# A hybrid gMLP/SSD layer on one core: rounded A parts kept in HBM, y's transposes and stores placed later, and the last three steps of the output projection run tile by tile

## The chip, the core and the metric

One core of a Trainium2 chip runs one launch of the kernel. The metric is the device time of an execution in microseconds (us); less is better. The engines are called as in the profile: PE (TensorE: matrix products and transposes), DVE (VectorE), ACT (ScalarE), POOL (GpSimd) and SP (SyncE, which issues every transfer of this kernel).

## What is computed

`x` is 2048 tokens by 1024 features, float32. The reference, cut to what matters here:

```python
h = rms_norm(x, pre_w)
proj = einsum('bld,dc->blc', h, w_in)            # 1024 -> 6160 columns
u, v, zg, z, xbc, dt_raw = split(proj)
# group A, 8 heads of 128: spatial gating in chunks of 128 tokens
s   = einsum('hts,bcshd->bcthd', tril(ws), layer_norm(v)) + bs
y_a = grouped_rms_norm(u * s * silu(zg), gmlp_norm_w, 128)
# group B, 16 heads of 64: causal conv, SiLU, Mamba-2 scan in chunks of 128
y   = y_diag + y_off + xs * d_skip
y_b = grouped_rms_norm(y * silu(z), ssd_norm_w, 256)
mixed = einsum('blc,cd->bld', concat([y_a, y_b]), w_out)   # 2048 -> 1024
out = x + rms_norm(mixed, post_w)
```

## The kernel before, in words

**Products.** The input projection is done as six units of 1024 columns (u = 0 to 5 in `UNITS`: xbc, z, xbc, v, u/zg, u/zg), the output projection as unit 6. Tokens are cut into four blocks of T = 512, handled as two pairs (`PAIRS`, p = 0 and 1); a block and half of the contraction is a quarter of a 2x2 block product, and each pair is done with seven products instead of eight (Winograd's form of Strassen's scheme): `PRODS` P1 to P7. The left operand A of a product is either a plain quarter of the activations (P1, P2, P4: `PLAIN_A`) or a sum or difference of quarters (P6, P7, P5, P3); the right operand B comes in the same way from the weights.

**Steps and tiles.** A step is one product on one slice j of the contraction: 28 steps in each of units 0 to 5, 56 in unit 6, 224 in all. A step runs over four tiles c of 128 rows; a tile is two calls of `mm3`, that is six products of 128x128 by 128x512. `mm3` gives fp32 accuracy from rounded parts: each operand is split into a part rounded to fp32r ("hi") and the rest ("lo"), and hi·hi, hi·lo and lo·hi are added. `split` (lines 157 to 162) makes the two parts of a 128x1024 piece: one ACT copy (line 160) and one DVE subtraction (line 161).

**Where A comes from.** `make_a` (line 720) makes the A of a step. In unit 0 it loads and combines pieces, splits them, and for the combined products stores both parts (1 MB) in HBM, in `a_d` (line 776). Units 1 to 5 use the same activations: for the combined products they load both parts from `a_d` with one 1 MB transfer into a buffer of `apool` (line 732); for the plain products they load the 0.5 MB piece into a buffer of `rpool` and split it once more (lines 724 to 728). Unit 6 works on y and splits everything. `look_ahead` (line 829) makes the A of step i+2 and the B of step i+3 while step i runs. `apool` has 3 buffers, `bpool` 5, `rpool` 7.

**Beside the products.** `run_tasks` advances generators between the tiles; `now` counts 1.36 per tile (`RUN`), and a generator says with `yield n` how much later it is due. The longest one is `ssd_stream` (line 474): 16 rounds, one for each block and head group, of which one has the transposes of x, B and C into a PSUM bank (`tok_x`, `tok_b`), the decays and exponentials on ACT, four chunks (`chunk`: products, state, y), and a norm. The normalised y of a round is turned by `y_tiles` (line 546): two times four PE transposes into one of the three banks of pool `ps`, an ACT copy out of it (line 554), and a store. In the kernel before these two parts of the round before are run at lines 504 and 512, between `tok_x(1)`, `tok_b` and the next decays. For group A `gate_out` (line 621) normalises with ACT, waits 8, and runs `y_tiles`.

**Accumulators.** Pool `pj` has five PSUM banks; `after` (line 864) empties or copies an accumulator when a product's last slice is done (line 872 is ACT's copy of P1 in mid-accumulation, lines 876 to 901 are DVE's, line 614 is ACT's SiLU).

**Stores.** `store` puts a store in a list and `flush` issues it on SP once `now` has moved on by `BEHIND` = 2.7, that is two tiles.

**Order.** The kernel is built with a scheduler that orders each engine's instructions by a simulated time line, with the program's order as priority: PE's tiles of a step may be taken in mixed order when one part of an operand is late, and SP's transfers can move. On the chip each engine then works through its own list in that order.

**The end.** The last product of unit 6 is P3 of pair 1, four steps (j = 0 to 3). `use_o` (line 672) takes each finished tile: sum of squares on ACT, times the weight on DVE, then (second half of a row) reciprocal root of the mean on POOL (line 173), two DVE operations on the two halves (line 689), and two stores. `bring` (line 695) loads what these need, tile by tile in the step before the last one (line 932).

Of the kernel before, what the change touches and what calls it, by code (L numbers as in the profile page):

```python
# [8 lines left out]
F32 = mybir.dt.float32  # L9
# [6 lines left out]
P = 128  # L16
# [11 lines left out]
EPS = 1e-6  # L28
RUN = 1.36
SPACE = 2.5  # L30
BEHIND = 2.7
LOOK_A = 2
LOOK_B = 3

# [17 lines left out]
def hybrid_kernel(ctx: ExitStack, tc: tile.TileContext, x, x_t, pre_w, w_u, w_o, w_dt,  # L52
# [27 lines left out]
    def rt(name):  # L80
# [2 lines left out]

    hd = [[dram.tile([P, 2, T], F32, name=f"hd{b}_{j}") for j in range(4)] for b in range(NB)]
    a_d = [{(m, j): dram.tile([P, 2, 2, T], F32, name=f"as{p}{m}{j}") for m in PRODS for j in range(2)
            if m not in PLAIN_A} for p in range(2)]
    s_d = {(p, m, j): dram.tile([P, 2, T], F32, name=f"s{p}{m}{j}") for p in range(2) for m in ("S2", "S3")
           for j in range(4)}
    t3_d = [dram.tile([P, 2, T], F32, name=f"t3{j}") for j in range(4)]
# [67 lines left out]
    def split(pool, name, t):  # L157

        w = pool.tile([P, 2, 2, T], F32R, name=name)
        nc.scalar.activation(w[:, :, 0, :], t, AF.Copy)  # L160
        nc.vector.tensor_tensor(w[:, :, 1, :], t, w[:, :, 0, :], ALU.subtract)  # L161
        return w
# [39 lines left out]
    def spawn(gen, delay=0):  # L202
        task = [now[0] + delay, gen]
        tasks.append(task)
        if delay == 0:
            advance(task)
        return task
# [19 lines left out]
    def flush(until):  # L227
        while stores and stores[0][0] <= until:
            _, dst, src, then = stores.pop(0)
            nc.sync.dma_start(out=dst, in_=src)  # L230
            if then:
                then()
# [241 lines left out]
    def ssd_stream():  # L474
        order = [(b, 2 * u + n) for u in range(2) for n in range(2) for b in range(NB)]

        def ready(b, g):
            return all((bb, g) in raw_in for bb in range(b + 1))

        cur, prev = Ssd(*order[0]), None  # L480
        for i in range(4):
            cur.load_raw(i)
            if i % 2:
                yield 5
                cur.conv(i - 1)
                yield 0
                cur.conv(i)
                yield 0
        cur.silus()
        for n in range(len(order) + 1):  # L490
            nxt = Ssd(*order[n + 1]) if n + 1 < len(order) else None
            if nxt:
                while not ready(nxt.b, nxt.g):
                    yield 5
            if cur:
                while (cur.b, cur.g // 2) not in zs_in:
                    yield 5
                for c in range(NT):
                    cur.load_e(c)
                cur.tok_x(0)  # L500
                yield 0
                cur.tok_x(1)
            if prev:
                next(prev.out, None)
            yield 0
            if cur:
                cur.tok_b()
                cur.decay(0)
                cur.decay(1)
                yield 0  # L510
            if prev:
                next(prev.out, None)
            if not cur:
                return
            if nxt:
                nxt.load_raw(0)
            cur.load_z(0)
            cur.decay(2)
            cur.decay(3)
            yield 0  # L520
            cur.exps()
            cur.load_z(1)
            yield 0
            cur.operands(0)
            yield 0
            for c in range(NT):
                if nxt:
                    nxt.conv(c)
                    if c + 1 < NT:
                        nxt.load_raw(c + 1)  # L530
                yield 0
                if c + 1 < NT:
                    cur.operands(c + 1)
                cur.chunk(c)
                if c + 2 < NT:
                    cur.load_z(c + 2)
                yield 0
            if nxt:
                nxt.silus()
            cur.norm()  # L540
            yield 0
            prev, cur = cur, nxt
# [78 lines left out]
    def gate_out(b, hp):  # L621
        yg, ss = gate[b, hp], g_ss[b, hp]
        r = rsqrt_mean(ss[:, :, :].rearrange("p c i -> p (c i)"), NT * 2, 1.0 / P, "g")
        for c in range(NT):
            for i in range(2):
                nc.scalar.activation(yg[c][:, i * P:(i + 1) * P], yg[c][:, i * P:(i + 1) * P], AF.Copy,  # L626
                                     scale=r[:, 2 * c + i:2 * c + i + 1])
        yield 8
        yield from y_tiles(b, yg, hp)


# [88 lines left out]
    def make_a(u, p, name, j):  # L720

        piece = lambda m, k: a_piece(u, p, m, k, j)
        tt = nc.vector.tensor_tensor
        if name in PLAIN_A:
            t, = load([piece(*PLAIN_A[name])])
            yield
            yield split(apool, "a", t)
            return
        if 0 < u < 6:
            yield  # L730
            w = apool.tile([P, 2, 2, T], F32R, name="a")
            nc.sync.dma_start(out=w[:, :, :, :].bitcast(F32), in_=a_d[p][name, j][:, :, :, :])
            yield w
            return
        if u == 0:
            yield
        if name == "P6":
            if u == 0:
                t, q, r = load([piece(0, 0), piece(1, 0), piece(1, 1)])
                tt(t, t, q, ALU.subtract)  # L740
                s3_in[p, j] = t
                tt(r, r, t, ALU.subtract)
                s2 = s2_in[p, j] = [gt("s2") for _ in range(2)]
                for kk in range(2):
                    nc.gpsimd.tensor_copy(s2[kk], r[:, kk, :])
                t = r
            else:
                q, t = load([piece(1, 1), s_d[p, "S3", j]])
                yield
                tt(t, q, t, ALU.subtract)  # L750
                store(s_d[p, "S2", j], t)
        elif name == "P7":
            if u == 0:
                t = s3_in.pop((p, j))
            else:
                t, q = load([piece(0, 0), piece(1, 0)])
                yield
                tt(t, t, q, ALU.subtract)  # L758
                store(s_d[p, "S3", j], t)
        elif name == "P5":  # L760
            t, q = load([piece(1, 0), piece(1, 1)])
            if u:
                yield
            tt(t, t, q, ALU.add)  # L764
        elif u == 0:
            t, = load([piece(0, 1)])
            s2 = s2_in.pop((p, j))
            for kk in range(2):
                tt(t[:, kk, :], t[:, kk, :], s2[kk], ALU.subtract)
        else:  # L770
            t, q = load([piece(0, 1), s_d[p, "S2", j]])
            yield
            tt(t, t, q, ALU.subtract)
        w = split(apool, "a", t)
        if u == 0:
            store(a_d[p][name, j], w[:, :, :, :].bitcast(F32))
        yield w
# [133 lines left out]
    spawn(prep(1), 1)  # L911
    spawn(prep(2), 16)
    spawn(prep(3), 30)
    accs = {}
    for i, (u, p, name, j, first, fin) in enumerate(steps):
        _, channels, _, nj = UNITS[u]
        at = i - 28 * u
        if at == 0:
            if u == 1:
                spawn(ssd_stream(), 4)  # L920
            if u == 3:
                row_w["v"] = row_weights(v_w)
            if u == 6:
                row_w["post"] = row_weights(post_w)
        for uu in (4, 5):
            for b, n, w in WANTED:
                if i == uu * 28 + w - 5:
                    spatial_task[b, 2 * (uu - 4) + n] = spawn(spatial(b, 2 * (uu - 4) + n), 1)
        look_ahead(i)
        A, B = made_a.pop(i), made_b[u, name, j]  # L930
        for c in range(NT):
            if u == 6 and name in ("P3", "P5") and j == nj - 2:
                bring(PAIRS[p][name == "P5"], c)
            if first:
                accs[c] = pj.tile([P, T], F32, name="acc", tag="pj")
            cs = slice(c * P, (c + 1) * P)
            for kk in range(2):
                a, b_ = A[:, kk], B[:, kk]
                st, en = first and kk == 0, fin and kk == 1
                if channels:  # L940
                    m = mm3(accs[c], b_[:, 0, cs], b_[:, 1, cs], a[:, 0, :], a[:, 1, :], st, en)
                else:
                    m = mm3(accs[c], a[:, 0, cs], a[:, 1, cs], b_[:, 0, :], b_[:, 1, :], st, en)
            step_end[:] = [m.ins]
            now[0] += RUN
            if j == nj - 1:
                after(u, p, name, c, accs[c])
            with tc.issue_after(step_end[0]):
                flush(now[0])
            run_tasks()  # L950
    assert not tasks
    flush(now[0] + 99)

# [41 lines left out]
```

## Time and profile before

| | |
|---|---|
| median of 3 runs | 1606.11 us (1606.04 to 1612.49) |
| profiled execution | 1609.79 us, of which 1608.0 us from first to last instruction (span) |
| PE busy | 1515.3 us, 94% of the span |
| DVE, ACT, POOL busy | 70%, 54%, 25% |
| transfers | 456.88 MB, mean 284 GB/s |

The units of the product loop begin at about 37, 248, 441, 642, 854, 1072 and 1279 us. The profile lists busy time by engine, a granted TensorE clock (1.00 is 2.4 GHz, 0.50 is 1.2 GHz), the waits of each engine with what released them, and the chain that ended last. A wait costs time only where it holds the engine that bounds the kernel, or something that engine will need.

### The profile page before, as it was taken

Reading aid. Unit: us, or ns where it says so; the run is one execution under the profiler, and the core shown is the slowest. Engines: PE = TensorE matmul, PEld = TensorE weight load, DVE = VectorE, ACT = ScalarE, POOL = GpSimd, SP = SyncE. Lnnn points to the kernel's source line nnn. Section 1 sums busy time; section 2 is a strip of 40 time slices with the busy share of each in tenths; the row PEclk is TensorE's granted clock in tenths of the full one; section 3 lists DMA queues with packets and bytes.
Section 4 is the critical chain, followed back from the end, with each engine's and each line's share of the span. In section 5 each row is a group of like instructions: output and inputs, shape, how many; then the busy total and the mean of one; then the engine's idle time right before and its main releaser. Section 6 shows DMA issues by size and latency. Waiting matters only on the chain. (4 is left out here: it accounts for less than half of the span.)

```text
span 1608.0 us, 21653 instructions
## 1 busy us (share of the span) xinstructions
PE 1515.3 (94%) x7268; PEld 1259.7 (78%) x7268; DVE 1129.0 (70%) x1756; ACT 870.8 (54%) x1823; POOL 408.7 (25%) x449
## 2 busy tenths in 40 slices
PE   4979999999989999999899899998999999999996
PEld 4768888778778888778778788787888887888875
DVE  4466876677676687677778669696676645687698
ACT  4431325666576654665466765879647743333332
POOL 1000000323332333342224434364624300000022
PEclk9987999999999999999999999999999999999998
DMA  8699999968788697786787776757866689797998
GB/s 334 251 365 348 334 416 337 343 224 285 273 274 291 222 328 273 255 300 238 259 285 233 251 268 217 260 175 250 293 222 233 216 278 331 259 380 247 336 357 327
DMA packets 159119, 456.88 MB, mean 284 GB/s; under 512 B 18848, under 2 KB 35616, under 8 KB 146720
## 3 DMA queue, kind: packets, MB, share of 16 engines
q1 hardware_dynamic: 159008, 455.51, 80.2%
q8 instruction: 57, 0.93, 0.2%
q14 instruction: 54, 0.44, 0.1%
HBM read 348.35 MB, written 107.09 MB: 283 GB/s over the span
## 5 line engine op out<-in xcount | busy, mean ns | idle before, releaser
L165 PE MATMUL acc<-b,a 128*128 128x512 f32 x1344 | 543.4, 405 | 19.7 <-ACT sg L614 4.9
L167 PE MATMUL acc<-b,a 128*128 128x512 f32 x1344 | 526.4, 396 | 4.6 <-DVE a L161 4.2
L166 PE MATMUL acc<-b,a 128*128 128x512 f32 x1344 | 528.7, 393 | 0.0
L165 PEld LDWEIGHTS acc<-b,a 128*128 128x128 f32 x1344 | 254.4, 189 | 75.0 <-ACT sg L614 5.5
L167 PEld LDWEIGHTS acc<-b,a 128*128 128x128 f32 x1344 | 254.1, 189 | 60.1 <-DVE a L161 5.9
L166 PEld LDWEIGHTS acc<-b,a 128*128 128x128 f32 x1344 | 254.9, 190 | 49.7
L160 ACT ACTIVATE a<-r 128x1024 fp32r<-128x1024 f32 x144 | 151.8, 1056 | 242.1 <-PE acc L167 115.6
L161 DVE TENSOR_TENSOR a<-r,a 128x1024 fp32r<-128x1024 f32 x144 | 179.0, 1244 | 70.1 <-ACT a L160 69.7
L165 PE MATMUL acc<-a,b 128*128 128x512 f32 x448 | 182.5, 415 | 16.6 <-ACT b L160 5.8
L372 DVE SCALAR_TENSOR_TENSOR cv_out<-cv_raw,cw,cv_out 128x512 f32<-128x512 f32 x192 | 161.2, 848 | 36.9 <-ACT cv_out L370 35.5
L166 PE MATMUL acc<-a,b 128*128 128x512 f32 x448 | 180.4, 403 | 0.5 <-DVE a L161 0.5
L167 PE MATMUL acc<-a,b 128*128 128x512 f32 x448 | 179.2, 404 | 0.0
L161 DVE TENSOR_TENSOR b<-r,b 128x1024 fp32r<-128x1024 f32 x112 | 144.2, 1290 | 40.8 <-ACT b L160 40.7
L160 ACT ACTIVATE b<-r 128x1024 fp32r<-128x1024 f32 x112 | 117.3, 1051 | 72.1 <-DVE r L815 17.5
L165 PEld LDWEIGHTS acc<-a,b 128*128 128x128 f32 x448 | 87.1, 195 | 37.1 <-ACT b L160 5.9
L184 ACT ACTIVATE junk<-y 128x128 bf16<-128x128 f32 (+1 forms) x192 | 65.5, 341 | 85.9 <-POOL y L465 72.5
L457 POOL TENSOR_TENSOR state<-state,ex 128x256 f32<-128x256 f32 x60 | 54.4, 906 | 217.6 <-PE y_ps L451 217.3
L166 PEld LDWEIGHTS acc<-a,b 128*128 128x128 f32 x448 | 87.3, 195 | 19.1 <-DVE a L161 1.0
L167 PEld LDWEIGHTS acc<-a,b 128*128 128x128 f32 x448 | 86.6, 193 | 18.8 <-issue 0.2
L436 POOL TENSOR_TENSOR xde<-xtok,dte 128x256 f32<-128x256 f32 x64 | 56.2, 884 | 158.5 <-ACT xtok L408 158.4
L173 POOL TENSOR_TENSOR o_r<-o_ms,mhalf 128x1 f32<-128x1 f32 x16 | 18.8, 1187 | 295.5 <-DVE o_ms L171 285.4
L389 ACT ACTIVATE E<-E,cs 128x128 f32<-128x128 f32 x256 | 79.9, 389 | 23.4 <-DMA E<-scr 23.3
(163 smaller groups left out, 2149.8 us busy)
## 6 DMA issues: line engine op xcount, KB each, us to landing
r<-w_u SPq DMA_DIRECT2D x108, 512.0 KB, 4.9
r<-hd SPq DMA_DIRECT2D x96, 512.0 KB, 5.6
a<-as0P SPq DMA_DIRECT2D x40, 1024.0 KB, 7.2
a<-as1P SPq DMA_DIRECT2D x40, 1024.0 KB, 7.0
r<-yd SPq DMA_DIRECT2D x72, 512.0 KB, 5.2
r<-w_o SPq DMA_DIRECT2D x36, 512.0 KB, 5.2
E<-scr SPq DMA_DIRECT2D x64, 256.0 KB, 6.7
yd<-yT SPq DMA_DIRECT2D x64, 256.0 KB, 3.3
```

The lines of the kernel that those rows point to most:

```text
L160: nc.scalar.activation(w[:, :, 0, :], t, AF.Copy)
L161: nc.vector.tensor_tensor(w[:, :, 1, :], t, w[:, :, 0, :], ALU.subtract)
L165: nc.tensor.matmul(dst, lhsT=a_hi, rhs=b_hi, start=first, stop=False, skip_group_check=True)
L166: nc.tensor.matmul(dst, lhsT=a_hi, rhs=b_lo, start=False, stop=False, skip_group_check=True)
L167: return nc.tensor.matmul(dst, lhsT=a_lo, rhs=b_hi, start=False, stop=last, skip_group_check=True)
L173: nc.gpsimd.tensor_tensor(r, ms, mhalf[:, 0:n], ALU.pow)
L184: nc.scalar.activation(junk[:, 0:n], src, AF.Square, accum_out=dst)
L372: nc.vector.scalar_tensor_tensor(cv, raw[:, j:j + T], cw[:, ti, j:j + 1], cv, ALU.mult, ALU.add)
L389: nc.scalar.activation(E[:, h, :], E[:, h, :], AF.Relu, scale=-1.0, bias=dts[self.b]["cs"][:, o + h:o + h + 1])
L436: nc.gpsimd.tensor_tensor(h4(xde[:, :]), xc, hv(d["dte"], g, c), ALU.mult)
L457: nc.gpsimd.tensor_tensor(h4(st[:, :]), h4(st[:, :]), ev(d["ex"], 1, g, c), ALU.mult)
```

## The change

Three edits. First, in unit 1 the split parts of the plain products are stored in `a_d` too, and in units 2 to 5 they are loaded from there, as the combined ones are. Second, the two parts of y's transposes run in the chunk loop of the next round (c = 0 and 1), for the last round after a wait of 8; `gate_out` waits 14 in place of 8; `BEHIND` is 5.4 in place of 2.7, for every store of the kernel. Third, the last three steps form one group: the loop runs over the tiles, and inside a tile over the three steps. With it the calls of `bring` of a step are made together, ahead of the step's `look_ahead`.

```diff
-BEHIND = 2.7
+BEHIND = 5.4
...
-            if m not in PLAIN_A} for p in range(2)]
+            } for p in range(2)]
...
-            if prev:
-                next(prev.out, None)
             yield 0
             if cur:
                 cur.tok_b()
                 cur.decay(0)
                 cur.decay(1)
                 yield 0
-            if prev:
-                next(prev.out, None)
             if not cur:
+                yield 8
+                for _ in prev.out:
+                    yield 0
                 return
...
                     if c + 1 < NT:
                         nxt.load_raw(c + 1)
+                if prev and c < 2:
+                    next(prev.out, None)
                 yield 0
...
-        yield 8
+        yield 14
         yield from y_tiles(b, yg, hp)
...
-        if name in PLAIN_A:
+        if name in PLAIN_A and not 1 < u < 6:
             t, = load([piece(*PLAIN_A[name])])
             yield
-            yield split(apool, "a", t)
+            w = split(apool, "a", t)
+            if u == 1:
+                store(a_d[p][name, j], w[:, :, :, :].bitcast(F32))
+            yield w
             return
...
+    LAST = 3
+    groups = [[i] for i in range(len(steps) - LAST)] + [list(range(len(steps) - LAST, len(steps)))]
...
+        if u == 6 and name in ("P3", "P5") and any(steps[n][3] == nj - 2 for n in group):
+            for c in range(NT):
+                bring(PAIRS[p][name == "P5"], c)
+        for n in group:
+            look_ahead(n)
+        made = [(made_a.pop(n), made_b[u, name, steps[n][3]], steps[n]) for n in group]
         for c in range(NT):
-            if u == 6 and name in ("P3", "P5") and j == nj - 2:
-                bring(PAIRS[p][name == "P5"], c)
...
+            for A, B, (_, _, _, j, first, fin) in made:
```

## Rows read from the trace of the kernel before

**Rows 1.** The page, busy us of each engine with share and count.
```profile
PE 1515.3 (94%) x7268; PEld 1259.7 (78%) x7268; DVE 1129.0 (70%) x1756; ACT 870.8 (54%) x1823; POOL 408.7 (25%) x449
```
**Rows 2.** Windows: length, busy of PE, PEld, DVE, ACT, POOL, clock, DMA share, GB/s.
```profile
441.00:642.00 201.00, 195.65 (x958) 162.11 (x957) 142.06 (x208) 118.96 (x228) 63.26 (x76) 0.99 0.82 277
642.00:854.00 212.00, 198.49 (x960) 163.63 (x958) 154.34 (x251) 125.33 (x233) 66.47 (x78) 0.98 0.78 267
854.00:1072.00 218.00, 208.91 (x1085) 175.68 (x1085) 167.72 (x289) 156.41 (x409) 96.42 (x104) 0.99 0.70 237
1072.00:1279.00 207.00, 200.99 (x1043) 169.53 (x1042) 141.85 (x248) 148.85 (x414) 88.18 (x89) 0.99 0.69 236
```
**Rows 3.** Waits of PE, 441 to 1279 us: waiter, releaser, total us, times, longest.
```profile
PE acc L165 <- ACT sg L614: 4.9, 2, 4.5
PE y_tp L552 <- ACT y L471: 4.5, 1, 4.5
PE acc L165 <- ACT p L872: 4.1, 1, 4.1
PE acc L165 <- DVE p L892: 3.9, 3, 3.1
PE acc L165 <- ACT a L160: 3.1, 1, 3.1
PE y_tp L552 <- ACT yT L554: 3.0, 3, 1.6
PE cb_ps L422 <- ACT xtok L408: 2.4, 1, 2.4
...
PE cb_ps L422 <- ACT yT L554: 1.0, 1, 1.0
...
PE acc L165 <- DMA a<-as0P: 0.6, 2, 0.4
```
**Rows 4.** Windows of 40 us, same columns as Rows 2.
```profile
760.00:800.00 40.00, 35.13 (x164) 28.96 (x163) 31.20 (x48) 22.17 (x31) 9.66 (x13) 0.91 0.70 234
1400.00:1440.00 40.00, 40.00 (x178) 33.14 (x177) 30.74 (x35) 14.12 (x19) 0.00 (x0) 1.00 1.00 386
```
**Rows 5.** Window of tile a alone: busy of PE, PEld, DVE, ACT; then clock, DMA.
```profile
441.00:1279.00 838.00, 675.34 (x2689) 500.57 (x2688) 61.14 (x48) 50.57 (x48) 0.99 0.74 254
```
**Rows 6.** Time line of ACT, 764 to 774 us: start, length, instruction.
```profile
768.96 1.04 ACT L160 ACTIVATE a<-r 128x1024 fp32r<-128x1024 f32 x1
...
771.33 1.70 ACT L471 ACTIVATE y<-y,s_r 128x256 f32<-128x256 f32 x4
```
**Rows 7.** Windows of all instructions, columns as Rows 2, for transfers.
```profile
200.00:240.00 40.00, 40.00 (x186) 33.40 (x185) 30.29 (x46) 10.36 (x10) 0.00 (x0) 1.00 1.03 415
240.00:320.00 80.00, 76.93 (x364) 63.82 (x363) 53.68 (x68) 48.06 (x78) 14.81 (x15) 1.00 0.94 341
```
**Rows 8.** Waits of SP's queue, 441 to 1279 us, columns as Rows 3.
```profile
SPq L230 <- ACT yT L554: 89.6, 34, 10.3
...
SPq L732 <- PE acc L167: 61.4, 30, 6.8
```
**Rows 9.** Time line, 1590 to 1610 us: start, length, instruction, wait before it.
```profile
1594.21 0.63 ACT L184 ACTIVATE junk<-p 128x512 bf16<-128x512 f32 x1 [5.83 <-DVE p L897]
1594.34 0.69 DVE L897 TENSOR_TENSOR p<-p,acc 128x512 f32<-128x512 f32 x1 [0.22 <-PE acc L167]
...
1595.73 0.39 PE L167 MATMUL acc<-b,a 128*128 128x512 f32 x1
...
1597.14 0.54 POOL L173 TENSOR_TENSOR o_r<-o_ms,mhalf 128x1 f32<-128x1 f32 x1 [9.01 <-DVE o_tot L178]
...
1598.54 0.92 POOL L173 TENSOR_TENSOR o_r<-o_ms,mhalf 128x1 f32<-128x1 f32 x1 [0.86 <-DVE o_ms L171]
...
1603.73 0.76 DVE L689 SCALAR_TENSOR_TENSOR xres<-p,o_r,xres 128x512 f32<-128x512 f32 x1
```
**Rows 10.** Wait of PE, 1279 to 1608 us, columns as Rows 3.
```profile
PE acc L167 <- DVE a L161: 3.7, 3, 2.0
```

More of the change, by code (lines that the diff above doesn't have):

```diff
@@ L913, in hybrid_kernel @@
     spawn(prep(3), 30)
+    LAST = 3
+    groups = [[i] for i in range(len(steps) - LAST)] + [list(range(len(steps) - LAST, len(steps)))]
     accs = {}
-    for i, (u, p, name, j, first, fin) in enumerate(steps):
+    for group in groups:
+        i = group[0]
+        u, p, name, j = steps[i][:4]
         _, channels, _, nj = UNITS[u]
@@ L928, in hybrid_kernel @@
                     spatial_task[b, 2 * (uu - 4) + n] = spawn(spatial(b, 2 * (uu - 4) + n), 1)
-        look_ahead(i)
-        A, B = made_a.pop(i), made_b[u, name, j]
+        if u == 6 and name in ("P3", "P5") and any(steps[n][3] == nj - 2 for n in group):
[4 more added lines that the diff above has]
+        made = [(made_a.pop(n), made_b[u, name, steps[n][3]], steps[n]) for n in group]
         for c in range(NT):
-            if u == 6 and name in ("P3", "P5") and j == nj - 2:
-                bring(PAIRS[p][name == "P5"], c)
-            if first:
-                accs[c] = pj.tile([P, T], F32, name="acc", tag="pj")
             cs = slice(c * P, (c + 1) * P)
[L937 to L950, printed above, removed]
+            for A, B, (_, _, _, j, first, fin) in made:
+                if first:
+                    accs[c] = pj.tile([P, T], F32, name="acc", tag="pj")
+                for kk in range(2):
+                    a, b_ = A[:, kk], B[:, kk]
+                    st, en = first and kk == 0, fin and kk == 1
+                    if channels:
+                        m = mm3(accs[c], b_[:, 0, cs], b_[:, 1, cs], a[:, 0, :], a[:, 1, :], st, en)
+                    else:
+                        m = mm3(accs[c], a[:, 0, cs], a[:, 1, cs], b_[:, 0, :], b_[:, 1, :], st, en)
+                step_end[:] = [m.ins]
+                now[0] += RUN
+                if j == nj - 1:
+                    after(u, p, name, c, accs[c])
+                with tc.issue_after(step_end[0]):
+                    flush(now[0])
+                run_tasks()
     assert not tasks
```

## The prediction, made before the changed kernel was run

> **What bounds the kernel now.** The page first: PE is busy 94% of the span, DVE 70%, ACT 54% [rows 1]. PE is the engine to look at, and since no edit takes products away, the change can only move PE's idle time, its clock, and what lies before and behind its first and last product. How fast PE goes when nothing holds it is seen in the output projection: 178 products in 40 us, 225 ns each, at a granted clock of 1.00 [rows 4].
>
> The windows by unit say how much there is to win. In units 2 to 5 PE is idle for 201 - 195.65 = 5.4, 212 - 198.49 = 13.5, 218 - 208.91 = 9.1 and 207 - 200.99 = 6.0 us, together 34 us [rows 2]. The clock column of the same four rows gives 2.0 + 4.2 + 2.2 + 2.1 = 10.5 us of TensorE time not granted [rows 2]. So units 2 to 5 hold some 44 us.
>
> Then PE's waits there. Hardly one of them is for a transfer (0.6 us); they are for ACT or DVE, which empty PSUM banks or make an operand [rows 3]. In two places this is the whole story. Around 770 us ACT has a split of A, other queued work and the normalisation of y to do, and y's transposes on PE wait 4.5 us for that normalisation [rows 3, 6]; in the 40 us around it the granted clock is 0.91, so 3.6 us more are gone at the 1.2 GHz level [rows 4]. And one wait of 3.1 us is for ACT's split of A itself [rows 3].
>
> **The change, part by part.**
>
> *y's transposes moved.* The waits in which y's transposes or their bank stand at either end are 4.5 (for y), 3.0 and 1.0 (for ACT's copy out of the bank): 8.5 us, with the 3.6 us of clock 12.1 us [rows 3, 4]. In the new place the norm of that round lies several generator turns back, so the 4.5 us wait should go. The transposes issue the same things as before: 8 PE transposes, two ACT copies and two stores a round. They are moved past `tok_b`, the decays, the exponentials and the first operands; on SP past the loads of raw and z. `tok_b`'s banks come free sooner, which bears on the 2.4 us wait of cb_ps as well [rows 3]. What they meet there is bounded from both sides below: at best -12 us, at worst the loss of the second rival. I take two thirds of the best, -8 us, since some of the bank waits will come back at the new place. `gate_out` waiting 14 in place of 8 is the same kind of move, with y held longer in a pool that v and z are loaded into; I count it in this term.
>
> *Stores later.* SP's queue stands for 89.6 us in units 2 to 5 with a store of yT that ACT hasn't made yet [rows 8], and every load behind it waits too. Two tiles more let most of that go. But PE waits 0.6 us for transfers [rows 3], so this is worth nothing on PE by itself: 0. Against it, a stored piece keeps its buffer two tiles longer; in unit 6, where each combined operand is stored out of `rpool`, late operands cost 3.7 us now [rows 10]. I bound this at -3 to +4 us and take +0.5.
>
> *Plain A parts.* In units 2 to 5 all 48 splits of A that ACT and DVE do are of plain pieces (12 a unit: 3 products, 2 slices, 2 pairs): ACT 50.57 us, DVE 61.14 us [rows 5]. All go. What comes instead is 48 transfers of 1 MB for 48 of 0.5 MB. None of that engine time is on PE; what it is worth is read from the waits for ACT and DVE at accumulators: 4.9, 4.1, 3.9, 3.1 us [rows 3], 16.0, and with what is left of the clock loss (10.5 - 3.6 = 6.9 us [rows 2, 4]) 22.9 us. The splits of P1 and P2 fall just where ACT must copy P1's accumulator (line 872) and empty it for SiLU (line 614), so a split of 1.04 us [rows 6] stands ahead of those copies. The 3.1 us wait should vanish; of the others, several us long against a split of 1.04, the split is a part, the rest being decays, exponentials and copies that stay. So 3.1, plus a third of the other 12.9, plus half of the 6.9 us of clock: -10.9, rounded to -10 us; the ends are -23 us and, if the new loads come late, +6. The new loads do wait on SP for a buffer of `apool`, whose present loads stand there 61.4 us in 30 waits, 2 us each [rows 8]; a buffer that comes free when a step ends is needed two steps later, over 10 us, and such loads hold PE for 0.6 us in all now.
>
> *Unit 1 pays.* It gains no relief and issues 12 more stores of 1.05 MB. Eight of them come from P1 and P2, in its first eight steps, the worst place: 240 to 320 us already moves 341 GB/s [rows 7]. Just ahead, 200 to 240 us moves 415 GB/s at a DMA share of 1.03, with PE busy for all 40 us [rows 7]; so 415 is what the transfers can do, and being there didn't hold PE. Room in these 80 us: 74 GB/s, 5.9 MB; wanted: 8.4 MB. The 2.5 MB over make 6 us of lateness at 415 GB/s, against operands fetched two steps ahead. Bounds 0 and +6, taken +1.5.
>
> *The end.* Now the last product ends at 1596.1 and the last DVE operation at 1604.5 us, 8.4 us later [rows 9], since four tiles finish within 4 us and each has some 3 us of DVE work. Tile by tile they finish three tile-times apart (18 products of 225 ns, 4 us), so DVE is done with three of them when the last comes. Left behind the last product: 0.69 on DVE, 0.63 on ACT, the root on POOL, two operations of 0.76, with hand-offs some 4.0 us [rows 9]. That is -4 us (0 to -5). The root took 0.54 us beside DVE's line 897, and 0.92 us beside its line 689 [rows 9]. The Trainium skill (SBUF — State Buffer, "A bandwidth-pool intuition that's wrong (but worth ruling out)") puts slowdowns like this down to a lock on a port that DVE and GpSimd share and not to shared bandwidth; by that rule the last root, with DVE idle, takes the short time, and with the long one the sum would be 0.4 us higher.
>
> *Group and `bring`.* Three steps' A must be there within three tiles where one was needed. PE can start other tiles' slices meanwhile, as the build's scheduler may order it; 12 loads of 256 KB in one go stand ahead of the step's operand loads on SP. Bounds 0 and +5, taken +1.
>
> Sum: -8 + 0.5 - 10 + 1.5 - 4 + 1 = -19 us. Against the profiled execution, 1609.8 us (span 1608.0 and 1.8 around it), that is 1590.8; the median of the runs lies 3.7 us below that execution, so 1587 us.
>
> **The rivals.**
>
> *The stalls only change place.* ACT's queue in units 2 to 5 stays more than half busy even without the splits, and the long waits are made of its table loads, decays and copies. A wait that loses 1 us of its backlog is then met by the next one in PE's own order. For it: the two longest groups, 4.9 and 4.1, are each mostly one wait [rows 3], against a split of 1.04 us. Against it: one wait is for the split itself. Then the end's -4 and -3 from the rest remain: 1599 us, within 0.5%.
>
> *Slower: the moved transposes hold PE in the chunk loop.* There `chunk` takes two of the three `ps` banks each time, and a transposing group needs the third, freed only by ACT's copy. When a copy is late now, PE stands 1.0 to 1.6 us [rows 3]. With 15 rounds and two groups in each, 30 such waits of 1 us would be +30 us in place of nothing, so -19 + 30 = +11: 1617 us. It decides from 0.6 us a group for no gain, and makes the kernel slower by more than 0.5% from 0.9 us. Against it: chunks lie several tiles apart, and the present waits for a copy are three [rows 3], and the code has 64 such groups (16 rounds and 16 gates, two each), most of them in units 2 to 5.
>
> *Unit 1's transfers bind.* The 6 us of lateness reach PE, and the clock falls behind the stall as at 770 us (3.6 us): +9.6 for +1.5, 1595 us. The Trainium skill (DMA: Bandwidth & Descriptors, "Where 436 GB/s comes from") would have about 358 GB/s bind between HBM and SBUF; by it (341 GB/s and the 8.4 MB against 358) the lateness would be 20 us and the time some 1608 us. The 415 GB/s over 40 us [rows 7] speaks against that limit here.
>
> **How the numbers follow.** A measurement of this kernel tells 0.5%, 8 us, from no change: under 1598 is faster, over 1614 slower. The forecast and what lies around it has 0.58; the stalls changing place 0.19; the chunk loop 0.10; unit 1's transfers 0.13, which still end on the fast side three times in four. Faster 0.69, same 0.20, slower 0.11. The likeliest case's own range is 1577 to 1597: with the best ends of the two big terms, -8 + 0.5 - 20 - 4 = near -30, and with half of them, -10. For 8 in 10 it reaches into the rival of no gain and part of the way to the slower one: 1574 to 1608.
>
> **What would show it.** In the changed profile, from 441 to 1279 us: no split of A on ACT in units 2 to 5, ACT some 50 and DVE some 60 us less busy; no wait of y's transposes for line 471; PE idle there down from 34 to about 20 us, and fewer windows under a clock of 0.98. In unit 1: GB/s near 415 in its first 80 us, and no PE wait for a transfer over 2 us. At the end: the last DVE operation some 4 us behind the last product. It is wrong if PE's idle time in units 2 to 5 stays near 34 us, if y_ps, st_ps or y_tp show a dozen waits near 1 us, or if unit 6 loses more than 5 us to late operands.

## The result, and the profile after

The changed kernel takes 1585.2 us (median of 4 runs, 1584.35 to 1587.56), the kernel before 1607.07 us (4 runs in all): a ratio of 0.986, 95% interval 0.9834 to 0.9885, and 21.9 us. The forecast was 1587 us, out of a range from 1574 to 1608. The profiled executions are 1584.35 and 1609.79 us, the spans 1582.6 and 1608.0.

The page after, busy us of each engine, to be read against [rows 1]:

```profile
PE 1508.9 (95%) x7268; PEld 1258.4 (80%) x7268; DVE 1068.9 (68%) x1708; ACT 819.8 (52%) x1769; POOL 390.1 (25%) x449
...
DMA packets 160847, 494.63 MB, mean 313 GB/s; under 512 B 19040, under 2 KB 35808, under 8 KB 140768
```

PE does the same 7268 products. DVE and ACT are some 60 and 51 us less busy, and 38 MB more are moved. What changed in PE's time is seen by stage, in the windows of the changed kernel for unit 1, units 2 and 3, and units 4 and 5 (columns as in [rows 2]):

```profile
244.00:439.00 195.00, 185.89 (x893) 154.70 (x892) 135.02 (x193) 111.59 (x203) 55.09 (x60) 0.98 0.98 373
439.00:829.00 390.00, 384.77 (x1912) 321.70 (x1910) 263.75 (x431) 215.29 (x435) 120.83 (x151) 1.00 0.88 314
829.00:1254.00 425.00, 412.87 (x2131) 348.33 (x2131) 281.21 (x514) 290.84 (x804) 175.56 (x197) 0.98 0.75 262
```

Units 2 and 3 went from 201 + 212 = 413 us [rows 2] to 390, at a clock of 1.00. Units 4 and 5 took 218 + 207 = 425 us before [rows 2], and 425 after. In finer steps, from the first product of a stage to the first of the next, the 25.4 us between the two spans divide into: start and unit 0 -3.5, unit 1 +1.4, units 2 and 3 -23.0, units 4 and 5 -0.2, unit 6 +0.3, behind the last product -0.4. So the gain has one place, and the question is which edit made it and why units 4 and 5 and the end gained nothing.

PE's waits after, units 2 to 5 and then unit 1 (columns as in [rows 3]):

```profile
PE y_ps L448 <- DVE xdt L434: 4.3, 1, 4.3
PE acc L165 <- DVE p L896: 2.8, 2, 2.4
PE acc L165 <- ACT p L876: 2.5, 1, 2.5
PE y_tp L553 <- DVE y L598: 1.7, 1, 1.7
PE y_tp L553 <- ACT xtok L408: 1.5, 1, 1.5
...
PE acc L165 <- DMA a<-as0P: 0.2, 1, 0.2
```
```profile
PE acc L165 <- DMA a<-as0P: 5.2, 1, 5.2
PE acc L165 <- ACT a L160: 3.5, 2, 2.7
```

The wait of y's transposes for the normalised y, and the one for ACT's split, are gone from units 2 to 5; the 4.3 and the 2.5 us lie in unit 5, the 2.4 us in unit 3. In unit 1 there is now a wait of 5.2 us for a transfer. Last, SP's queue at stores of yT, units 2 to 5 (columns as in [rows 8]):

```profile
SPq L230 <- ACT yT L555: 71.7, 27, 7.3
```

### The profile page after: what moved, and what is told of

It reads as the page before. It is cut to its first block, busy times and chain, and to the rows that moved or that the text cites. A ratio compares the mean times of both kernels' runs of the same rounds, so it can differ in the third digit from the quotient of the medians.

```text
span 1582.6 us, 21521 instructions
## 1 busy us (share of the span) xinstructions
PE 1508.9 (95%) x7268; PEld 1258.4 (80%) x7268; DVE 1068.9 (68%) x1708; ACT 819.8 (52%) x1769; POOL 390.1 (25%) x449
## 4 chain that ended last, share of the span: by engine, by line
PE 57%; DMA 13%; DVE 11%; ACT 7%; issue 3%; POOL 1%; SPq 1%; DVEq 0%; ACTq 0%; POOLq 0%
PE acc L165 16%; PE acc L167 16%; PE acc L166 16%; DMA E<-scr 3%; DMA r<-yd 3%; PE y_ps L448 3%; ACT E L389 2%; DMA r<-w_o 2%; PE y_ps L451 1%; PE st_ps L453 1%; DVE cv_out L372 1%; DVE a L161 1%; PE s_ps L594 1%; PE y_tp L553 1%; DVE b L161 1%
## 5 line engine op out<-in xcount | busy, mean ns | idle before, releaser
L160 ACT ACTIVATE a<-r 128x1024 fp32r<-128x1024 f32 x96 | 101.1, 1057 | 200.8 <-PE acc L167 88.5
L372 DVE SCALAR_TENSOR_TENSOR cv_out<-cv_raw,cw,cv_out 128x512 f32<-128x512 f32 x192 | 155.1, 810 | 41.5 <-ACT cv_out L370 39.5
L161 DVE TENSOR_TENSOR a<-r,a 128x1024 fp32r<-128x1024 f32 x96 | 117.3, 1223 | 50.5 <-ACT a L160 50.3
L457 POOL TENSOR_TENSOR state<-state,ex 128x256 f32<-128x256 f32 x60 | 46.9, 781 | 239.5 <-PE y_ps L451 239.4
L436 POOL TENSOR_TENSOR xde<-xtok,dte 128x256 f32<-128x256 f32 x64 | 52.3, 824 | 165.0 <-ACT xtok L408 158.7
```

What stands on the lines that cost most here:

```text
L372: nc.vector.scalar_tensor_tensor(cv, raw[:, j:j + T], cw[:, ti, j:j + 1], cv, ALU.mult, ALU.add)
L436: nc.gpsimd.tensor_tensor(h4(xde[:, :]), xc, hv(d["dte"], g, c), ALU.mult)
L457: nc.gpsimd.tensor_tensor(h4(st[:, :]), h4(st[:, :]), ev(d["ex"], 1, g, c), ALU.mult)
```

## The experiments

All ratios are to the kernel before, run beside each kernel; its medians there were 1608.09 us (the three edits alone and the early A), 1610.95 us (later stores with the plain parts, the gate, 25 buffers) and 1606.03 us (the rest). The changed kernel run again beside the second of these is the yardstick.

> The changed kernel itself, as the yardstick for the kernels run beside it: 1585 us, ratio to before 0.986.

It came to 1586.6 us, 0.9853 (0.9831 to 0.9875): two measurements of one kernel agree within 0.1%.

**Each edit alone.** The first edit on the kernel before:

```diff
-        if name in PLAIN_A:
+        if name in PLAIN_A and not 1 < u < 6:
...
+            if u == 1:
+                store(a_d[p][name, j], w[:, :, :, :].bitcast(F32))
```

> Only the first edit: plain A parts stored in unit 1 and loaded in units 2 to 5. The stated working (-10 us there, +1.5 us in unit 1) gives about 1598 us against 1607 (ratio 0.995). If the gain of the whole change is mainly the splits, 1588 to 1594 and PE idle in units 2 to 5 falls from 34 us to under 20. If the stalls only change place, or later stores make the gain, within 4 us of 1607.

Measured 1594.23 us, 0.992 (0.9902 to 0.9939), -13.9 us. The second edit alone:

```diff
-BEHIND = 2.7
+BEHIND = 5.4
...
-            if prev:
-                next(prev.out, None)
...
+                if prev and c < 2:
+                    next(prev.out, None)
...
-        yield 8
+        yield 14
```

> Only the second edit: y's transposes in the chunk loop, the gate's wait of 14, stores after 5.4. The stated working (-8 +0.5) gives about 1599 us (ratio 0.995); the wait of y's transposes for line 471 (4.5 us) gone. If the moved transposes hold PE in the chunk loop: 1607 or more, with a dozen waits near 1 us at y_tp, y_ps or st_ps. If this edit makes the whole gain: about 1586.

Measured 1614.8 us, 1.0048 (1.0031 to 1.0065): slower, by 6.7 us. The third alone:

```diff
+    LAST = 3
+    groups = [[i] for i in range(len(steps) - LAST)] + [list(range(len(steps) - LAST, len(steps)))]
...
+            for A, B, (_, _, _, j, first, fin) in made:
```

> Only the third edit: last three steps in one group. The stated working gives -3 us, 1604, with 8.0 us or so from the last product to the end of the span. The rival, that the group changes nothing because the last step's A is late: each engine works through the same list as before, 1607 within 1 us, and 12 us from the last product to the end of the span.

Measured 1606.06 us, 0.9988 (0.9971 to 1.0005): no change. ACT, DVE, POOL and SP get the same instructions in the same order with and without this edit. PE's order differs in some 20 products between 1583 and 1588 us, which belong to the steps before the last one. The last step's 24 products come in the same order in both: two for each of the four tiles, which need only the rounded part of A, then the other four of each. So the tiles end four products apart either way. The build's scheduler takes PE's tiles by when their operands come, and the order of the loop doesn't change that for the last step.

Alone, the three give -13.9 + 6.7 + 0 = -7 us; together -21.9. The first two are worth some 15 us more together than apart. The stages show where (us per stage, from first product to first product, unit 6 to its last product; profiled executions):

| | unit 1 | units 2, 3 | units 4, 5 | unit 6 |
|---|---|---|---|---|
| before | 193.4 | 412.5 | 425.5 | 316.3 |
| plain A parts alone | 208.2 | 389.7 | 422.1 | 315.3 |
| plain A parts, stores later | 195.5 | 386.9 | 437.4 | 319.5 |
| second edit alone | 191.7 | 402.3 | 438.0 | 317.1 |
| all (changed) | 194.8 | 389.4 | 425.3 | 316.6 |

A stage of one execution is good to some 4 us: with the third edit alone, whose lists are those of the kernel before up to 1583 us, the first three columns are 193.3, 408.6 and 428.0, and the changed kernel run again has 195.4, 389.1 and 426.1. So the first edit is worth 19 to 23 us in units 2 and 3. The second alone, which leaves every split of A in place, takes 6 to 10 us off there too, and together with the first it adds nothing to that.

The third row is a run of its own, the first edit with `BEHIND` alone:

```diff
-BEHIND = 2.7
+BEHIND = 5.4
```

> The kernel before with the plain parts kept and stores 5.4 late; transposes and gate as before. With the plain parts alone unit 1 lost 14 us to transfers (loss 25 in place of 11 us). If later stores alone take that back, as the whole change did: 1584 to 1587, and unit 1 lasts 195 us, not 208. If it was the moved transposes: 1594, as with the first edit alone.

Measured 1597.46 us, 0.9921 (0.9903 to 0.9938): in total not clearly other than without the later stores, yet in other stages. In unit 1 they are worth 208.2 - 195.5 = 12.7 us, in units 4 and 5 they cost 437.4 - 422.1 = 15.3. (The profiled execution of the second edit alone was its shortest, 1607.5 us against a median of 1614.8, so its row flatters it; that of the first edit with later stores was its longest, 1599.56 us.)

Unit 1 first. With the plain parts alone, its windows, PE's waits, SP's waits from 246 to 320 us, and then window and SP's waits of the changed kernel from 244 us:

```profile
240.00:320.00 80.00, 71.74 (x307) 58.35 (x306) 44.27 (x54) 48.52 (x74) 8.51 (x9) 0.91 0.93 360
247.00:455.00 208.00, 193.99 (x902) 160.67 (x901) 141.14 (x198) 128.73 (x224) 59.36 (x64) 0.95 0.93 348
```
```profile
PE acc L165 <- DMA a<-as0P: 6.8, 3, 4.1
PE acc L165 <- ACT a L160: 4.2, 3, 2.7
PE y_ps L451 <- DVE state L458: 3.0, 1, 3.0
```
```profile
SPq L230 <- ACT stage L637: 16.0, 6, 6.0
SPq L230 <- DVE a L161: 12.7, 6, 2.6
```
```profile
240.00:320.00 80.00, 70.89 (x318) 57.63 (x317) 48.85 (x61) 43.32 (x69) 10.21 (x9) 0.96 1.02 395
```
```profile
SPq L230 <- DVE a L161: 10.0, 5, 3.5
SPq L230 <- ACT stage L638: 6.5, 7, 2.9
```

With stores two tiles behind, SP's queue stands 28.7 us before a store whose data isn't made, with the next operands' loads behind it; the transfers reach 360 GB/s, and the whole unit runs at a clock of 0.95. Four tiles behind, that standing is 16.5 us, the same window moves 395 GB/s at a share of 1.02, and the unit's clock is 0.98. The run with the later stores alone beside the plain parts agrees: 14.9 us and 392 GB/s. SP's waits in all come to about the same, 41.3 and 43.5 us, but 24.6 of the second are for transfers under way, against 4.8 of the first. On PE the 12.7 us are idle time (14.0 us with the plain parts alone, 9.7 with the later stores) and, for the larger part, clock (5% of 208 us against 2% of 195). That later stores do this is shown; that they do it through SP's queue is read from these waits.

Units 4 and 5 with the plain parts alone, then with the stores later too but the transposes in their old place, windows and PE's waits of the second:

```profile
844.00:1267.00 423.00, 410.79 (x2129) 344.25 (x2128) 284.27 (x510) 293.68 (x806) 175.74 (x192) 1.00 0.75 262
829.00:1266.00 437.00, 416.84 (x2135) 349.76 (x2135) 286.46 (x513) 301.77 (x813) 173.29 (x196) 0.98 0.73 254
```
```profile
PE acc L165 <- ACT p L875: 8.0, 2, 6.8
PE s_ps L593 <- DVE cbm L424: 2.9, 1, 2.9
PE y_ps L448 <- DVE yo L463: 2.5, 1, 2.5
```

PE waits 6.8 us at once for ACT's copy of P1. In the second edit alone (waits of units 2 to 5) it waits 8.4 us at once for DVE in unit 5, and 6.7 us at once for ACT's copy of P1 in unit 2:

```profile
PE y_ps L448 <- DVE xdt L434: 8.4, 1, 8.4
PE acc L165 <- ACT p L873: 8.2, 3, 6.7
PE acc L165 <- ACT sg L615: 5.2, 2, 3.6
```

These are single long waits, not many short ones. Of the 15.3 us about half is PE's idle time (20.2 us against 12.2), and about as much is clock (0.98 against 1.00). With the transposes and `gate_out` moved as well, units 4 and 5 are back at 425. So that move is worth 12 us there, but of a loss that the later stores brought, and most of it is the gate's: with `gate_out` back at 8 and all else as changed (below), the median is 1593.93 us, between 1597.46 and the yardstick's 1586.6. That leaves 7.3 us to the gate's wait and 3.5 us to the transposes, which is within the noise. How a later store leads to ACT's or DVE's late work there isn't settled; that the buffers it holds longer change the order in which the build places work is only argued. Plain parts with moved transposes and no later stores wasn't tried.

**Is it engine time?** The forecast priced the plain parts by the time that ACT and DVE no longer spend. Two kernels give that time back without putting it between a load and a product: behind each load of a plain A in units 2 to 5, one ACT copy, or one DVE subtraction, of 128x1024 of it, whose result nothing uses.

```diff
+            if name in PLAIN_A:
+                nc.scalar.activation(spare, w[:, :, 0, :].bitcast(F32), AF.Copy)
```

> The changed kernel, with one ACT copy of 128x1024 put back for each of the 48 loaded plain A parts (its result isn't used), 1.0 us each. If ACT's time is what the first edit gives back: the loss in units 2 and 3 goes from 10 us back towards the 33 us of before, and the time towards 1600. If it is DVE's time or the transfers' path: within 5 us of 1585.

```diff
+            if name in PLAIN_A:
+                nc.vector.tensor_tensor(spare, w[:, :, 0, :].bitcast(F32), w[:, :, 1, :].bitcast(F32), ALU.subtract)
```

> The same with one DVE subtraction of 128x1024 for each of the 48 loaded parts (result not used), 1.2 us each, and no ACT copy. If DVE's time is the gain: units 2 and 3 lose some 20 us more than in the changed kernel. If ACT's: within 5 us of 1585.

Measured 1590.24 us, 0.9888 (0.9864 to 0.9912), and 1594.62 us, 0.9908 (0.9872 to 0.9944). Their added rows (min/median/max in ns) stand for the 48 splits that the change removed [rows 5]; then the windows of units 2 and 3 with ACT's time back, and of units 2, 3 and of 4, 5 with DVE's:

```profile
L738 ACT ACTIVATE spare<-a x48: 1039/1057/1078, 437.7 to 1184.3; 128x1024 bf16<-128x1024 f32 x48
```
```profile
440.00:829.00 389.00, 385.57 (x1910) 322.53 (x1908) 265.62 (x432) 235.76 (x456) 131.00 (x152) 1.00 0.89 315
```
```profile
L738 DVE TENSOR_TENSOR spare<-a x48: 1171/1226/1761, 437.3 to 1194.0; 128x1024 bf16<-128x1024 f32 x48
```
```profile
439.00:827.00 388.00, 384.59 (x1908) 322.50 (x1907) 297.34 (x457) 212.06 (x433) 133.40 (x151) 1.00 0.89 316
827.00:1264.00 437.00, 417.68 (x2134) 352.20 (x2133) 310.07 (x536) 289.29 (x802) 181.71 (x197) 0.97 0.74 255
```

Units 2 and 3 stay at 389 and 388 us, though ACT is busy for 236 us (244.3 before the change), or DVE for 297 (296.4 before). In the first kernel the added copies even stood at the head of ACT's queue, waiting for their load, and PE lost nothing by it:

```profile
ACT spare L738 <- DMA a<-as1P: 15.8, 6, 5.7
...
ACT spare L738 <- DMA a<-as0P: 7.9, 4, 2.8
```

So the gain of units 2 and 3 is not the time of either engine alone; both at once wasn't tried. What remains is the split's place: an A that is loaded doesn't pass through ACT's and DVE's queues before PE may use it, and the build orders the rest differently for it. Which of these two it is, the runs don't tell apart. In units 4 and 5, the kernel with DVE's time back took 437 - 425 = 12 us longer. This was one of the longer of its four executions (1587.96 to 1598.76 us); its median is some 8 us above the yardstick. So DVE's time counts there, by an amount that isn't settled. The 4 us or so by which the kernel with ACT's time back lies above the yardstick show in no stage up to unit 5 of its profile, which was its shortest execution.

**What holds units 4 and 5.** In the changed kernel unit 4 takes 203 us and unit 5 222; before, 218 and 207 [rows 2]. This was read as the scan's products bunching up behind `qpool`'s 22 full buffers. Two tries: `gate_out` letting go of its y sooner, and three more buffers.

```diff
-        yield 14
+        yield 8
```

> The changed kernel with the gate's wait back at 8. If what the changed kernel loses from 1032 to 1254 us (10 us of PE idle and 13.7 us at half clock, after a stretch in which the 22 buffers of qpool are all taken and the scan stands still) comes from group A's y being held longer: that stretch gives back 6 to 10 us, 1576 to 1579. If the moved transposes of the scan hold the pool, or if it is chance: within 3 us of the yardstick.

```diff
-    qpool = ctx.enter_context(tc.tile_pool(name="qpool", bufs=22))
+    qpool = ctx.enter_context(tc.tile_pool(name="qpool", bufs=25))
```

> The changed kernel with 25 buffers of qpool in place of 22, nothing else. If a full qpool is what stops the scan in units 4 and 5: 4 to 10 us less, with the half clock between 1032 and 1254 us gone or cut. If qpool is not the cause: within 3 us of the yardstick.

Measured 1593.93 us, 0.9898 (0.9873 to 0.9922), and 1583.21 us, 0.9842 (0.982 to 0.9864), against the yardstick's 0.9853. The windows of units 4 and 5, first with 8, then with 25 buffers:

```profile
827.00:1258.00 431.00, 414.76 (x2140) 349.05 (x2139) 283.48 (x515) 295.15 (x810) 179.04 (x198) 0.98 0.75 259
```
```profile
827.00:1252.00 425.00, 412.67 (x2136) 348.06 (x2135) 287.17 (x514) 291.32 (x804) 180.91 (x197) 0.98 0.76 262
```

Holding y longer is right, by some 7 us of the medians (the profiled execution with 8, 1586.11 us, was its shortest), and the theory that it costs buffers fell. With 25 buffers unit 5 loses some 6 us less in PE's idle time and clock and unit 4 some 7 more; the sum stays at 425. The pool moves the loss and doesn't make it.

**Unit 1's transfers.** P2's parts stored in unit 2 in place of unit 1, alone and with 25 buffers:

```diff
+        kept = 2 if name == "P2" else 1
-        if name in PLAIN_A and not 1 < u < 6:
+        if name in PLAIN_A and not kept < u < 6:
...
-            if u == 1:
+            if u == kept:
```

> The changed kernel with only P2's parts kept in unit 2 in place of unit 1. By the room counted for transfers (5.9 MB for 8.4 wanted, now 4.2), PE's wait of 5.2 us for a loaded A in unit 1 goes, with its 6.8 us at half clock: unit 1 lasts 189 to 192 us, not 195; unit 2 gets 4 splits back. 1581 to 1584. If unit 1's wait comes from SP's order and not from the bytes: 195 us again.

> The changed kernel with 25 buffers of qpool, and P2's plain parts kept in unit 2 in place of unit 1 (split once more in unit 2). If both costs are as read: 2 us less from qpool, and half of unit 1's 8.4 MB of early stores gone, so that its loss falls from 13 to about 9 us while unit 2 loses 1 to 2 more: 1580 to 1582. If not: 1583 to 1586.

Measured 1584.58 us, 0.986 (0.9835 to 0.9884), and 1581.62 us, 0.9841 (0.9814 to 0.9868). Windows of the first:

```profile
240.00:320.00 80.00, 74.47 (x342) 61.21 (x341) 51.31 (x67) 42.82 (x71) 12.61 (x14) 0.98 0.98 374
243.00:434.00 191.00, 185.37 (x892) 154.34 (x892) 131.90 (x189) 115.33 (x207) 52.46 (x60) 0.99 0.94 344
434.00:826.00 392.00, 385.43 (x1909) 322.31 (x1907) 274.38 (x437) 216.48 (x436) 130.62 (x152) 1.00 0.90 324
```

What is moved in the 80 us falls from 395 to 374 GB/s, the 5.2 us wait is gone, and unit 1 is 4 us shorter; units 2 and 3 are 3 us longer, which is no more than two executions can differ there. So a third less to store in unit 1 ends that wait; whether the cost of the stores is then paid in unit 2 isn't shown. Both versions lie below or at the changed kernel, but within its interval: no version here beats it clearly.

**The end.** The last step's A made four steps earlier, into a free buffer of `bpool`:

```diff
+EARLY = 6
...
+        if i == len(steps) - EARLY:
+            load_a(*end)
+            do_a(*end)
+            early.add(end[0])
...
+        w = split(bpool, "b", t) if at_end else split(apool, "a", t)
```

> The changed kernel, with the last step's A made four steps earlier (its loads, difference and split are placed at step 218), in the one buffer of bpool that is free by then. If the group's gain at the end is held up by that A alone, the last four tiles finish over 2 us apart, and the end shrinks by 2 to 3 us against the changed kernel: 1582 to 1583. If DVE's work behind the tiles sets the end whatever PE's order, no difference: 1585.

Measured 1591.39 us, 0.9906 (0.9888 to 0.9924): 5 to 6 us slower than the changed kernel. Time lines of the end (columns as in [rows 9]), first of the changed kernel:

```profile
1565.27 1.22 DVE L161 TENSOR_TENSOR a<-r,a 128x1024 fp32r<-128x1024 f32 x1
...
1570.73 0.39 PE L167 MATMUL acc<-b,a 128*128 128x512 f32 x1
...
1571.98 0.68 DVE L901 TENSOR_TENSOR p<-p,acc 128x512 f32<-128x512 f32 x1
...
1578.74 0.75 DVE L690 SCALAR_TENSOR_TENSOR xres<-p,o_r,xres 128x512 f32<-128x512 f32 x1
```

Then with the early A, and PE's waits in its unit 6, and last those in unit 6 of the changed kernel:

```profile
1574.77 0.69 DVE L913 TENSOR_TENSOR p<-p,acc 128x512 f32<-128x512 f32 x1
...
1578.24 0.68 DVE L913 TENSOR_TENSOR p<-p,acc 128x512 f32<-128x512 f32 x1
...
1578.87 0.39 PE L168 MATMUL acc<-b 128*128 128x512 f32 x1
...
1582.86 1.05 POOL L174 TENSOR_TENSOR o_r<-o_ms,mhalf 128x1 f32<-128x1 f32 x2 [3.19 <-DVE o_ms L172]
...
1583.44 0.75 DVE L691 SCALAR_TENSOR_TENSOR xres<-other,o_r,xres 128x512 f32<-128x512 f32 x1 [0.59 <-POOL o_r L174]
...
1585.43 0.75 DVE L691 SCALAR_TENSOR_TENSOR xres<-p,o_r,xres 128x512 f32<-128x512 f32 x1
```
```profile
PE acc L168 <- DVE a L162: 5.6, 4, 1.9
PE acc L166 <- ACT a L161: 4.5, 3, 1.8
```
```profile
PE acc L167 <- DVE a L161: 3.8, 3, 2.0
```

In the changed kernel the last step's A is finished on DVE at 1566.49 us (1565.27 + 1.22), 4.6 us before the last product's end, behind the outputs of earlier tiles in DVE's list; all four tiles must wait for it, and so they still finish together. With A early, PE does finish the tiles one by one, ten products (2.3 us) apart, and the last DVE operation ends 1586.18 - 1579.26 = 6.9 us behind the last product's end, against 1579.49 - 1571.12 = 8.4. But other steps' A come later for it: PE's waits for them in unit 6 are 10.1 us for 3.8 (6.6 in the changed kernel's second profile), and unit 6 is 2 to 4 us longer. The rest of the loss isn't explained: 5 us of it lie in units 4 and 5 of this execution (430.5 us), where every engine's list is the changed kernel's.

## Why the prediction was right, and where its sum was not

The total was right, -22 us by the medians against -19, and three of its signs showed. It was in good part luck: the terms behind it were off, and partly cancelled. PE's idle time in units 2 to 5 is 815 - 384.77 - 412.87 = 17.4 us against 34 [rows 2], for a forecast of about 20. ACT is 43 and DVE 61 us less busy there, and the wait of y's transposes for y is gone. Three signs failed: unit 1's first 80 us moved 395 GB/s for 415, with a wait of 5.2 us for a transfer where none over 2 us should be, and the last DVE operation is 8.4 us behind the last product, not 4.

- *Plain A parts, -10.* The right edit, for a reason that wasn't borne out: -19 to -23 us in units 2 and 3, nothing clear of noise in units 4 and 5. The term counted a third of the waits for ACT and DVE [rows 3], reasoning from a split of 1.04 us [rows 6]. Giving either engine its time back returned none of that, so the step that failed is pricing the splits by the engine that a wait named. What took its place, an operand that passes no engine's queue or another order of the build, stays open. The same edit also cut into the wait that was credited to the moved transposes: with the plain parts alone, PE waits for the normalised y 2.8 us in units 2 and 3, in four waits, for 4.5 in one [rows 3].
- *y's transposes, -8.* Not shown. The second edit alone is 6.7 us slower, and the move gains 12 us only where the later stores lose 15, some 7 of the 12 by the gate's wait, which the term counted as a side matter. That the loss is made of some 30 short waits of PE, as the slower rival had it, is not so: long single ones do it.
- *Stores later, +0.5.* The step "this is worth nothing on PE by itself" failed. It was true of the kernel before, where PE waits 0.6 us for transfers [rows 3], and was carried over to unit 1, which the same change fills with stores: there it is worth 12.7 us. It also costs 15.3 us in units 4 and 5, which no step looked at; the bound of +4 was for unit 6. Nor did two tiles more "let most of that go": in units 2 to 5 SP's queue still stands 71.7 us, in 27 waits, for ACT's yT, against 89.6 [rows 8].
- *Unit 1 pays, +1.5.* Together with the later stores +1.4; the first edit alone pays 14.8. The forecast had the lateness from bandwidth, (8.4 - 5.9) MB, and left the stores' delay out, which decides between the two. The rival of unit 1's transfers is right in its place: a wait of 5.2 us for a transfer, and a clock of 0.96 over the 80 us where it was 1.00 [rows 7]. Yet the unit as a whole lost only 1.4 us. The Trainium skill's limit of about 358 GB/s (DMA: Bandwidth & Descriptors, "Where 436 GB/s comes from") did not bind: 395 GB/s over the 80 us.
- *The end, -4, and the group, +1.* Neither shows (-0.4 us behind the last product). The step that failed is "tile by tile they finish three tile-times apart": it read the loops as the order on the chip, though the scheduler orders tiles by when operands come, and the last A comes late. The root's price is seen with the early A: the last two roots take 1.05 us together, 0.54 each, against 0.92 for one beside DVE [rows 9]. DVE is idle for the first alone. Beside the second, line 691 runs, begun 0.07 us after it; the root of 0.92 us began 0.23 us after such an operation. So what counts here is not that DVE is idle, as the forecast said, but which of the two begins first.
- *The stalls only change place.* True of units 4 and 5, where the chance given to it (0.19) was for the whole kernel; not of units 2 and 3.

## What to carry to other kernels

Two edits can be worth much more, or less, together than apart: price each against the kernel that the others leave, above all where one adds work to a queue and another changes when that queue stands. A wait names the engine that came last; whether that engine's time is the cost shows only when the time is given back. In a queue that issues in order, a store issued before its data is made delays every load behind it. And before a loop is reordered, look at whether the build keeps the program's order at all: here the last step came out in the same order.

## What was not expected of the hardware

ACT standing at the head of its queue for a transfer, 15.8 + 7.9 us in units 2 and 3, cost PE nothing, in a stage where ACT is busy 60% of the time (235.76 of 389 us). And a stream of loads and stores of one core reached 395 GB/s over 80 us, close to the 415 of [rows 7], once its queue stood less for data not yet made (16.5 us for 28.7).
